# One layer of a hybrid decoder: q and k groups as plain block products, branch sums collected in DRAM by adding DMAs, a new order of the seven products

## The chip, the cores and the metric

The kernel runs on one core of a Trainium2 chip. The metric is device time in microseconds (us) of one execution. The kernel before was timed three times: 840.45, 841.55 and 841.84 us, a median of 841.55 us.

A core has five engines that run their own instruction streams and wait for each other by semaphores: TensorE (PE in the profile; its weight loads are listed apart as PEld), VectorE (DVE), ScalarE (ACT), GpSimd (POOL) and SyncE (SP), which here only issues DMAs. Matmuls write PSUM, of which the kernel uses eight banks of 128 partitions x 512 fp32 values: four for the dense products (pool `pp`) and four for everything else (pool `pa`). The inputs, the weights and the output lie in DRAM; all else is in SBUF.

## The reference

The input is 512 tokens of width 1024 with 16 learned meta tokens ahead. One layer, with batch 1, then a final norm:

```
u = rms_norm(h)                              # 528 tokens x 1024
rq, rk, rv, rg, gq, gk, gv, gg, glr, m_ret, m_gla = split(u @ w_in)
# retention, 4 heads: q, k of 256, v of 512
o_ret = group_norm(retention(rope(rq), rope(rk) / 16, rv)) * silu(rg)
# gated linear attention, 4 heads: q, k of 128, v of 256
log_a = log_sigmoid(glr @ w_gate_up + b_gate) / 16
o_gla = rms_norm(gla(gq / sqrt(128), gk, gv, log_a)) * silu(gg)
merged = sigmoid(m_ret) * (o_ret @ w_branch_ret) + sigmoid(m_gla) * (o_gla @ w_branch_gla)
out = rms_norm(h + merged @ w_out)           # the 16 meta positions dropped
```

All of it is fp32. The wide products are u @ w_in (1024 x 11,280), the two branch products and w_out.

## The kernel before

**Splits.** TensorE multiplies fp32 values that are rounded to a shorter form (`fp32r`). To keep the accuracy, every operand is split in two parts, hi and lo: ScalarE writes hi as a rounded copy and VectorE writes lo = value - hi (`split`, lines 139-141). One product then takes three matmuls, hi*hi, hi*lo and lo*hi (`mm3`, lines 143-146, and the inner loop of `quad`, line 221).

**quad (lines 186-273).** Most groups of w_in columns are computed two 256-column blocks at a time, for both halves of the tokens, with seven block products in place of eight (Strassen's scheme in Winograd's form). Products are numbered 1 to 7; each is 24 matmuls. The token side of the seven (two plain blocks of u, sums of blocks, ...) is split once and kept: `fh[0..6]` and `fl[0..6]`. The weight side needs block sums that VectorE makes in place (lines 251, 252, 253, 259), and then a split. A product accumulates in a PSUM bank, b, a or c, and intermediate values are copied out of bank b by ScalarE (`copy`, line 228, tiles `*_x1` to `*_x3`) before the next product adds to that same bank. The order is 1 2 7 6 5 3 4: b gets 1, then 6, then 5, then 3. Between 6 and 5, and between 5 and 3, no other product stands on TensorE. VectorE adds the copies to the banks in the evacuation.

The q and k columns of a head (of a pair of heads in the gated part) are done `wide`: the matrix of weights is stationary, the tokens move, and the result is transposed. There the meta tokens ride along, so that each matmul moves 264 columns (256 tokens and 8 meta tokens), and a product has two banks. There are six such calls: gq0, gq1 and rq0 to rq3.

**Stages.** In order: norm and transposes of u (`xt`, line 411); gv0 (`proj_b`, with 512 columns a matmul); gq0 with the forget gates woven in (glr, z, la); gg0 with the attention of the first pair of gated heads; gq1; gv1; gg1 and the branch product bg0 (`branch`) with the attention of the second pair; bg1. Then for each retention head h: rq (woven with the attention of head h-1, tiles av, on, sg, ot), the branch product br of head h-1, rg woven with the scores (sc), and rv. At the end the gates mr0, mr1 (woven with the attention of head 3), mg0, mg1, then br3 and w_out.

**weave (from line 156).** It alternates one step of a dense generator (a product) with one step of a chain generator (attention). `ret_attention` has the steps values 0, 1, 2, turn 0, values 3, turn 1. `values(ib)` makes 128 tokens of the output (av), its norm on VectorE, GpSimd and ScalarE, and multiplies it into sg (line 874). `turn` transposes two such blocks on TensorE (ot, line 337), which reads sg.

**What sets the order.** The program is written as above, but a framework orders the instructions of each engine itself by a cost model, subject to the data dependences. In the kernel before it may move matmuls of one product ahead of others, and it does at some places.

**Buffers.** Raw weights, hi and lo parts have small rings (three for hi and lo); SyncE issues a weight load when its buffer is free. `acc` holds the sum of the gated branch in SBUF (1024 x 512 fp32, 16 KB a partition), `acc2` that of the retention branch. VectorE adds each branch product to them (lines 720 and 931). The gated sum goes to DRAM (`kept`) and is read back for the gates (`kp`). The gates: VectorE and ScalarE form the sigmoid, VectorE multiplies (906, 917), GpSimd adds to acc2 (918), and br3 adds the last product to it on VectorE (935).

## Time and profile before

| what | value |
|---|---|
| runs of the kernel before | 840.45, 841.55, 841.84 us |
| the profiled execution: time, span of its trace | 841.58 us, 839.8 us |
| granted TensorE clock, mean | 0.988 of full speed |
| PE busy | 784.0 us (93% of the span), 5322 matmuls |
| DVE, ACT, POOL busy | 619.5, 422.8, 133.7 us |
| DMA engines busy | 30%, 78.82 MB moved |
| gv0 begins, gq0 begins, gg0 begins | 11.1, 43.7, 82.2 us |
| TensorE begins to wait for turn 0 of head 0, 1, 2 | 367.8, 472.8, 578.0 us |

How to read it: the page gives busy time by engine, then the span in 40 slices with the TensorE clock that was granted, then the chain of work that ended last, then groups of instructions by line, then DMAs. In a row of groups or of the timeline stand the start, the duration, the engine, the line of the kernel, the operation, the tile written and the tiles read, the shape, and in brackets how long the engine had been idle and who released it. Matmuls overlap: a matmul of 256 columns is shown as 0.28 us long, but the next starts 0.12 us after it, so the cost of a row of matmuls is read from one start to the next.

### The profile page before, as it was taken

To read this page: it belongs to the slowest core of one execution; us is meant where nothing else is said; L and a number is where in the kernel's file an instruction comes from. 1 tells how busy PE (TensorE), PEld (TensorE's weight loads), DVE (VectorE), ACT (ScalarE), POOL (GpSimd) and SP (SyncE) were. 2 spreads that over 40 slices of the span, in tenths; PEclk is the share of its full clock that TensorE was granted. 3 is DMA by queue.
4 is the path that set the end of the run, shared out by engine and by line. 5 is a ranking of instruction groups with operands and counts; after the bars stand their busy time and mean duration, and the time that the engine had idled before them with its cause. 6 is when DMAs were issued, how large, how long until landed. Compare 5 with 4: busy or idle time off the path is not lost. (4 is left out here: it accounts for less than half of the span.)

```text
span 839.8 us, 13348 instructions
## 1 busy us (share of the span) xinstructions
PE 784.0 (93%) x5322; PEld 703.9 (84%) x5322; DVE 619.5 (74%) x893; ACT 422.8 (50%) x707; POOL 133.7 (16%) x170
## 2 busy tenths in 40 slices
PE   7987989999899989999999999999999998989996
PEld 4777888898787978987999879998799998888886
DVE  3889686777637698887677887788877877887822
ACT  6665775456742445545445443454434555454422
POOL 4500332022400130022000220002200000032031
PEclk8998999999999999999999999999999999999999
DMA  8212211224122504242222422224222236335202
GB/s 278 84 56 76 76 45 54 66 90 126 52 75 100 177 25 127 77 125 75 69 81 79 126 76 64 81 83 127 76 64 82 82 105 208 114 103 176 73 1 101
DMA packets 72390, 78.82 MB, mean 94 GB/s; under 512 B 6964, under 2 KB 64564, under 8 KB 72328
## 3 DMA queue, kind: packets, MB, share of 16 engines
q1 hardware_dynamic: 72328, 77.97, 30.5%
q8 instruction: 42, 0.69, 0.3%
q14 instruction: 20, 0.16, 0.1%
HBM read 73.77 MB, written 4.19 MB: 93 GB/s over the span
## 5 line engine op out<-in xcount | busy, mean ns | idle before, releaser
L152 POOL TENSOR_TENSOR g_r<-g_v,mhalf 128x1 f32<-128x1 f32 x16 | 10.1, 630 | 305.7 <-DVE g_v L151 305.7
L144 PE MATMUL br_p<-oh,br_h 128*128 128x512 f32 x128 | 50.7, 401 | 1.0 <-ACT br_h L140 1.0
L145 PE MATMUL br_p<-ol,br_h 128*128 128x512 f32 x128 | 50.3, 396 | 0.0
L146 PE MATMUL br_p<-oh,br_l 128*128 128x512 f32 x128 | 50.1, 395 | 0.0
L140 ACT CAST rg_h<-rg_w 128x1024 fp32r<-128x1024 f32 x24 | 25.3, 1052 | 45.8 <-PE br_p L145 24.2
L140 ACT CAST rq_h<-rq_w 128x1024 fp32r<-128x1024 f32 x24 | 25.3, 1053 | 34.4 <-PE bg_p L145 13.0
L221 PE MATMUL rv_b<-rv_h,fh 128*128 128x256 f32 x128 | 37.0, 289 | 3.5 <-ACT rv_x L228 3.5
L221 PE MATMUL rq_b<-fh,rq_h 128*128 128x264 f32 x128 | 36.9, 288 | 1.0 <-ACT rq_x L228 1.0
L141 DVE TENSOR_TENSOR rg_l<-rg_w,rg_h 128x1024 fp32r<-128x1024 f32 x24 | 29.3, 1221 | 11.3 <-ACT rg_h L140 11.3
L221 PE MATMUL rg_b<-rg_h,fh 128*128 128x256 f32 x128 | 36.6, 286 | 0.9 <-DVE rp L760 0.9
L221 PE MATMUL rq_b<-fh,rq_l 128*128 128x264 f32 x128 | 36.6, 286 | 0.0
L221 PE MATMUL rq_b<-fl,rq_h 128*128 128x264 f32 x128 | 36.3, 283 | 0.0
L221 PE MATMUL rv_b<-rv_l,fh 128*128 128x256 f32 x128 | 36.0, 281 | 0.0
L221 PE MATMUL rg_b<-rg_l,fh 128*128 128x256 f32 x128 | 36.0, 281 | 0.0
L221 PE MATMUL rv_b<-rv_h,fl 128*128 128x256 f32 x128 | 36.0, 281 | 0.0
L221 PE MATMUL rg_b<-rg_h,fl 128*128 128x256 f32 x128 | 35.9, 281 | 0.0
L141 DVE TENSOR_TENSOR rv_l<-rv_w,rv_h 128x1024 fp32r<-128x1024 f32 x24 | 29.0, 1222 | 8.0 <-ACT rv_h L140 7.8
L141 DVE TENSOR_TENSOR rq_l<-rq_w,rq_h 128x1024 fp32r<-128x1024 f32 x24 | 30.4, 1266 | 3.9 <-ACT rq_h L140 3.9
L140 ACT CAST rv_h<-rv_w 128x1024 fp32r<-128x1024 f32 x24 | 24.8, 1053 | 12.2 <-DVE rv_w L252 5.6
L144 PEld LDWEIGHTS br_p<-oh,br_h 128*128 128x128 f32 x128 | 23.8, 188 | 8.2 <-ACT br_h L140 1.2
L221 PEld LDWEIGHTS rv_b<-rv_h,fh 128*128 128x128 f32 x128 | 24.1, 188 | 7.3 <-ACT rv_x L228 6.1
L145 PEld LDWEIGHTS br_p<-ol,br_h 128*128 128x128 f32 x128 | 24.1, 188 | 5.9
(478 smaller groups left out, 3062.1 us busy)
## 6 DMA issues: line engine op xcount, KB each, us to landing
rq_w<-in_w_in_dram SPq DMA_DIRECT2D x16, 512.0 KB, 3.7
rg_w<-in_w_in_dram SPq DMA_DIRECT2D x16, 512.0 KB, 3.6
rv_w<-in_w_in_dram SPq DMA_DIRECT2D x16, 512.0 KB, 3.7
br_w<-in_w_branch_ret_dram SPq DMA_DIRECT2D x16, 512.0 KB, 3.4
gv_w<-in_w_in_dram SPq DMA_DIRECT2D x8, 512.0 KB, 7.4
gq_w<-in_w_in_dram SPq DMA_DIRECT2D x8, 512.0 KB, 4.0
gg_w<-in_w_in_dram SPq DMA_DIRECT2D x8, 512.0 KB, 3.8
bg_w<-in_w_branch_gla_dram SPq DMA_DIRECT2D x8, 512.0 KB, 3.5
```

The source lines that it names most:

```text
L140: nc.scalar.copy(hi, src)
L141: eng.tensor_sub(lo, src, hi.bitcast(F32))
L144: nc.tensor.matmul(o, lh, rh, start=first, stop=False)
L145: nc.tensor.matmul(o, lh, rl, start=False, stop=False)
L146: nc.tensor.matmul(o, ll, rh, start=False, stop=last)
L152: nc.gpsimd.tensor_tensor(r[:rows], v[:rows], mhalf[:rows], op=ALU.pow)
L221: nc.tensor.matmul(ps, l, r, start=first and j == 0, stop=last and j == 2, skip_group_check=not fresh or (t == 1 and not wide))
```

## The change

It has five parts.

1. **q and k groups.** The six wide calls of `quad` become two calls each of a new function, `proj_a`: plain block products, four (two halves of the depth by two halves of the tokens), each for two 128-column tiles and 4 x 3 matmuls, 96 matmuls for the 256 columns of q and 96 for those of k. q moves 256 columns (no meta tokens), k 264. Two weight splits for each in place of seven for both; no block sums, no copies out of PSUM, no adds. The rope reads the PSUM banks directly, for q in one set of 512-column operations.
2. **Order of the products in quad.** 1 2 6 7 5 4 3 in place of 1 2 7 6 5 3 4. The third intermediate is copied from bank c after product 7, no longer from b after 5. The second block sum is now t2.
3. **Order on TensorE.** `pin` ties the first matmul of each dense group to the last one of the group before (no semaphore, order only). Dense groups (gv, quad, proj_a, branch, w_out) then stand in program order; matmuls of the chains may still be placed between.
4. **Branch sums.** acc and acc2 go away. ScalarE copies each branch product out of PSUM, and a DMA stores it (the first term, by SyncE) or adds it in DRAM (later terms, by GpSimd with `accum_op=add`) to `kept` or `kept2`. 32 adding DMAs of 256 KB: 8 in bg1, 16 in br1 and br2, 8 in mg. In mr the sum is read, multiplied and written back; in mg `kept` is read, multiplied and added; in br3 `kept2` is read. GpSimd's scratch for descriptors grows from 1024 to 4096.
5. **Smaller ones.** In ret_attention both turns come after all four values. The forget gates use other buffers, and their last logarithm is five operations of 512 columns in place of one of 2560. The temporary ring `tmp` has 7 buffers in place of 6, the second pool of the gated part is gone, and the splits of one block of u stay all through.

The diff, cut:

```diff
+    order = []
+    def pin(ins):
+        if order:
+            tc.add_manual_dep(ins.ins, order[0].ins.name, mybir.DependencyInfo(
+                mybir.DependencyClass.NoSync, mybir.DependencyReason.DATA), reason="order of products")
+    def mm3(o, lh, ll, rh, rl, first, last, dense=False):
+        m = nc.tensor.matmul(o, lh, rh, start=first, stop=False)
+        if dense:
+            pin(m)
         nc.tensor.matmul(o, lh, rl, start=False, stop=False)
-        nc.tensor.matmul(o, ll, rh, start=False, stop=last)
+        m = nc.tensor.matmul(o, ll, rh, start=False, stop=last)
+        if dense:
+            order[:] = [m]
...
+        b, a, c = [ppt(f"{name}_{x}").rearrange("p (t c) -> p t c", t=2) for x in "bac"]
+        def product(i, form, w, ps, fresh):
             hi, lo = wsplit([P, 4, 256], f"{name}_{i}")
             split(hi, lo, w)
...
+                        if t == kk == j == 0:
+                            pin(m)
+            order[:] = [m]
 
...
-        product(1, A11, blk[0, 0], "b", True)
-        x1 = copy("b", 1)
+        product(1, A11, blk[0, 0], b, True)
+        x1 = copy(b, 1)
         run_late()
         yield
         t2 = wraw(f"{name}_t2")
-        product(2, A12, blk[1, 0], "a", True)
+        product(2, A12, blk[1, 0], a, True)
         nc.vector.tensor_sub(blk[0, 0], blk[0, 1], blk[0, 0])
+        nc.vector.tensor_sub(t2, blk[1, 1], blk[0, 0])
+        evac(0, 0, a, x1)
+        yield
+        product(6, S2, t2, b, False)
+        x2 = copy(b, 2)
         nc.vector.tensor_sub(blk[0, 1], blk[1, 1], blk[0, 1])
-        nc.vector.tensor_sub(t2, blk[1, 1], blk[0, 0])
-        out(0, 0, "a", x1)
-        yield
-        product(7, S3, blk[0, 1], "c", True)
-        yield
-        product(6, S2, t2, "b", False)
+        yield
+        product(7, S3, blk[0, 1], c, True)
+        x3 = copy(c, 3)
         nc.vector.tensor_sub(blk[1, 0], blk[1, 0], t2)
-        x2 = copy("b", 2)
         if meta is not None:
             late.append(lambda: meta(psm))
         yield
-        product(5, S1, blk[0, 0], "b", False)
-        out(1, 1, "c", copy("b", 3))
+        product(5, S1, blk[0, 0], b, False)
+        evac(1, 1, b, x3)
         run_late()
         yield
-        product(3, S4, blk[1, 1], "b", False)
-        out(1, 0, "b", None)
-        yield
-        product(4, A22, blk[1, 0], "c", False)
-        out(0, 1, "c", x2)
-        yield
+        product(4, A22, blk[1, 0], c, False)
+        evac(0, 1, c, x2)
+        yield
+        product(3, S4, blk[1, 1], b, False)
+        evac(1, 0, b, None)
+        yield
+    def proj_a(col, meta, name, evac):
+        if meta:
+            pss = [[ppt(f"{name}_p{t}{th}")[:, :HT] for th in range(2)] for t in range(2)]
+        else:
+            full = [ppt(f"{name}_p{t}") for t in range(2)]
+            pss = [[p[:, th * 256:(th + 1) * 256] for th in range(2)] for p in full]
+        n = HT if meta else 256
+        for kh in range(2):
+            raw = wraw(f"{name}_w{kh}")
+            hi, lo = wsplit([P, 4, 256], f"{name}_{kh}")
+            nc.sync.dma_start(raw, w_in[kh * 512:kh * 512 + 512, col:col + 256].rearrange("(k p) c -> p k c", p=P))
+            split(hi, lo, raw)
+            for th in range(2):
+                for t in range(2):
+                    c = slice(t * P, t * P + P)
+                    for kk in range(4):
+                        a = [f[th, kh][:, kk, :n] for f in (ah, al)]
+                        first = kh == kk == 0 and (meta or th == 0)
+                        for j, (l, r) in enumerate(((hi, a[0]), (hi, a[1]), (lo, a[0]))):
+                            m = nc.tensor.matmul(pss[t][th], l[:, kk, c], r, start=first and j == 0,
+                                                 stop=kh == 1 and kk == 3 and j == 2,
+                                                 skip_group_check=not meta and th == 1)
+                            if t == kk == j == 0:
+                                pin(m)
+                order[:] = [m]
+                if meta and kh == 1:
+                    evac(th, [pss[t][th] for t in range(2)])
+                run_late()
+                yield
+        if not meta:
+            evac(full)
...
-        def evac(n, th, t, x, y):
-            if n == 1:
-                total(k[:, t, th, :], x, y)
-            else:
-                total(q[:, t, th * 256:(th + 1) * 256], x[:, :256], y if y is None else y[:, :256])
-        yield from quad((C_GQ + p * 256, C_GK + p * 256), False, f"gq{p}", evac, wide=True)
+        def evac_q(ps):
+            for t in range(2):
+                nc.scalar.copy(q[:, t, :], ps[t])
+        def evac_k(th, ps):
+            for t in range(2):
+                nc.vector.tensor_copy(k[:, t, th, :], ps[t])
+        yield from proj_a(C_GQ + p * 256, False, f"gq{p}", evac_q)
+        yield from proj_a(C_GK + p * 256, True, f"gk{p}", evac_k)
...
+    def collect(dst, t, first):
+        if first:
+            nc.sync.dma_start(dst, t)
+        else:
+            nc.gpsimd.dma_start(dst, t, accum_op=ALU.add)
 
     def gla_branch(p):
         def evac(c, ps):
-            if p == 0:
-                nc.scalar.copy(acc[:, c, :], ps)
-            else:
-                nc.vector.tensor_add(acc[:, c, :], acc[:, c, :], ps)
-                nc.sync.dma_start(kept[:, c, :], acc[:, c, :])
+            t = gp.tile([P, 512], F32, tag="gb", name=f"gb{p}{c}", bufs=2)
+            nc.scalar.copy(t, ps)
+            collect(kept[:, c, :], t, p == 0)
 
...
-        yield from quad((C_RQ + h * 256, C_RK + h * 256), False, f"rq{h}", evac, wide=True)
+        def evac_q(ps):
+            rope(ps, cs[:, 0, :, :256], cs[:, 1, :, :256], [qh[:, i, :] for i in range(2)],
+                 [ql[:, i, :] for i in range(2)], f"rpq{h}")
+        def evac_k(th, ps):
+            rope(ps, cs[:, 0, th, :], cs[:, 1, th, :], [kh[:, i, th, :] for i in range(2)],
+                 [kl[:, i, th, :] for i in range(2)], f"rpk{h}{th}")
+        yield from proj_a(C_RQ + h * 256, False, f"rq{h}", evac_q)
+        yield from proj_a(C_RK + h * 256, True, f"rk{h}", evac_k)
...
...
-        values(2)
-        yield
-        turn(sg, 0, oh, ol, rgain, h * 4, f"ot{h}")
-        yield
-        values(3)
-        yield
-        turn(sg, 1, oh, ol, rgain, h * 4, f"ot{h}")
-        yield
+        for ib in range(NTB):
+            values(ib)
+            yield
+        for half in range(2):
+            turn(sg, half, oh, ol, rgain, h * 4, f"ot{h}")
+            yield
...
+        def part(dst, src, g, name, first):
+            k = tmp2(name)
+            nc.sync.dma_start(k, src)
+            nc.vector.tensor_mul(k, k, g)
+            collect(dst, k, first)
...
-                a = acc2[:, 4 * j + 2 * n:4 * j + 2 * n + 2, s]
-                nc.vector.tensor_mul(a, a, g)
...
+                part(kept2[:, d, s], kept2[:, d, s], g, f"kr{j}{n}{th}", True)
...
-                nc.vector.tensor_mul(g, g, k)
-                nc.gpsimd.tensor_add(acc2[:, d, s], acc2[:, d, s], g)
...
+                part(kept2[:, d, s], kept[:, d, s], g, f"kg{j}{n}{th}", False)
...
     def ret_branch(h):
         def evac(c, ps):
-            if h == 0:
-                nc.scalar.copy(acc2[:, c, :], ps)
-            elif h < 3:
-                nc.vector.tensor_add(acc2[:, c, :], acc2[:, c, :], ps)
+            t = tmp(f"mt{h}{c}")
+            if h < 3:
+                nc.scalar.copy(t, ps)
+                collect(kept2[:, c, :], t, h == 0)
             else:
-                t = tmp(f"mt{c}")
+                k = tmp(f"mk{c}")
+                nc.sync.dma_start(k, kept2[:, c, :])
                 nc.vector.tensor_mul(t, sigr[c // 2][:, c % 2, :], ps)
-                nc.vector.tensor_add(t, t, acc2[:, c, :])
+                nc.vector.tensor_add(t, t, k)
                 split(mh[c // 2][:, c % 2, :], ml[c // 2][:, c % 2, :], t)
```

What the change does to the order of instructions, at three places.

**TensorE at the start.** Rows of TensorE's stream: xt0 to xt4 are the transposes of the five token blocks (the fifth is the meta tokens); gv0_p0 to p3 are the first product's four token tiles, and gv0_0, gv0_1, gv0_2 are consecutive quarters of its weights. Before, from the last matmul of p1 with the first quarter on (six matmuls of p1 with the second quarter follow these rows):

```order
L146 MATMUL gv0_p1_337<-gv0_0_h_341,fl0_87 128x512
L145 MATMUL gv0_p0_336<-gv0_1_l_372,fh0_80 128x512
L146 MATMUL gv0_p0_336<-gv0_1_h_371,fl0_87 128x512
L144 MATMUL gv0_p0_336<-gv0_1_h_371,fh0_80 128x512
L145 MATMUL gv0_p0_336<-gv0_1_l_372,fh0_80 128x512
L146 MATMUL gv0_p0_336<-gv0_1_h_371,fl0_87 128x512
```

Now, from the same place:

```order
L156 MATMUL gv0_p1_334<-gv0_0_h_338,fl0_87 128x512
L444 MATMUL xt2_0_214<-ident_71,xn2_212 128x128 x4
L444 MATMUL xt2_1_222<-ident_71,xn2_212 128x128 x4
L152 MATMUL gv0_p2_335<-gv0_0_h_338,a21h_101 128x512
L444 MATMUL xt3_0_239<-ident_71,xn3_237 128x128 x4
L444 MATMUL xt3_1_247<-ident_71,xn3_237 128x128 x4
L155 MATMUL gv0_p2_335<-gv0_0_l_339,a21h_101 128x512
```

The matmuls with the second quarter no longer stand ahead of the transposes of the third token block. Counted to the transposes xt4, 36 matmuls of gv0 stood ahead before and 19 stand there now.

**ScalarE in mg1.** ScalarE's stream, in which every product shows as the cast of its weights (mg1_1_h for product 1), with the copies out of PSUM between. Before:

```order
L140 CAST mg1_6_h_7958<-mg1_t2_7889 128x1024
L228 COPY mg1_x1_7887<-mg1_b0_7862 128x512
L140 CAST mg1_5_h_7989<-mg1_w00_7850 128x1024
L894 ACTIVATE mg100_7924<-mg100_7924 128x512
L140 CAST mg1_3_h_8026<-mg1_w11_7856 128x1024
L140 CAST mg1_4_h_8060<-mg1_w10_7852 128x1024
L228 COPY mg1_x2_7987<-mg1_b0_7862 128x512
L140 CAST br3_0_h_8110<-br3_0_w_8109 128x1024
L228 COPY mg1_x3_8017<-mg1_b0_7862 128x512
```

Now:

```order
L140 CAST mg1_7_h_7936<-mg1_w01_7830 128x1024
L140 CAST mg1_5_h_7967<-mg1_w00_7826 128x1024
L929 ACTIVATE mg100_7898<-mg100_7898 128x512
L140 CAST mg1_4_h_8002<-mg1_w10_7828 128x1024
L234 COPY mg1_x2_7933<-mg1_b_7834 128x512
L140 CAST mg1_3_h_8037<-mg1_w11_7832 128x1024
L234 COPY mg1_x3_7964<-mg1_c_7836 128x512
L140 CAST br3_0_h_8086<-br3_0_w_8085 128x1024
L929 ACTIVATE mg111_7995<-mg111_7995 128x512
```

All three copies came out of bank b; now the third comes out of bank c. x2 is copied while product 7 runs in bank c, and x3 while product 5 runs in b; the copies stood between two products of the same bank before.

**TensorE in rq1.** The second turn of head 0 (ot0_10 and ot0_11, each four transposes). Before, it stood in the last product of the wide quad (rq1_4):

```order
L221 MATMUL rq1_c1_3831<-fl2_89,rq1_4_h_4066 128x264
L221 MATMUL rq1_c1_3831<-fh2_82,rq1_4_l_4067 128x264
L337 MATMUL ot0_10_4048<-ident_71,sg0_3143 128x128 x3
L337 MATMUL ot0_11_4057<-ident_71,sg0_3143 128x128 x3
L221 MATMUL rq1_c1_3831<-fh2_82,rq1_4_h_4066 128x264
```

Now it stands in the middle of the k group:

```order
L297 MATMUL rk1_p11_3899<-a21l_102,rk1_0_h_3901 128x264
L297 MATMUL rk1_p11_3899<-a21h_101,rk1_0_l_3902 128x264
L372 MATMUL ot0_10_3972<-ident_71,sg0_3131 128x128 x4
L372 MATMUL ot0_11_3981<-ident_71,sg0_3131 128x128 x4
L297 MATMUL rk1_p00_3896<-fh1_81,rk1_1_h_3991 128x264
```

Between the last matmul of av03 and the second turn stood 42 matmuls of products 3 and 4 before; now there are 48 of the k group and the first turn. Between av01 and the first turn there were 48 matmuls of rq1, and now there are 72.

More of the change, by code (lines that the diff above doesn't have):

```diff
@@ L184, in wsplit, with quad @@
                 wp.tile(shape, F32R, tag="wlo", name=f"{name}_l", bufs=3))
-    def quad(cols, rows, name, evac, meta=None, wide=False):
+    def quad(cols, rows, name, evac, meta=None):
         blk = {}
@@ L199, in quad @@
                                   .rearrange("(k p) c -> p k c", p=P))
-        n_tok = HT if wide else 512
-        banks = {}
-        def bank(x):
-            banks[x] = [(pat if wide and x == "a" else ppt)(f"{name}_{x}{t}") for t in range(2 if wide else 1)]
-        def product(i, form, w, x, fresh):
+        b, a, c = [ppt(f"{name}_{x}").rearrange("p (t c) -> p t c", t=2) for x in "bac"]
+        def product(i, form, w, ps, fresh):
             hi, lo = wsplit([P, 4, 256], f"{name}_{i}")
@@ L219, in product @@
                     for j, (x1, x2) in enumerate(((0, 0), (0, 1), (1, 0))):
-                        l, r = (a[x1], b[x2]) if rows else (b[x1], a[x2])
-                        nc.tensor.matmul(ps, l, r, start=first and j == 0, stop=last and j == 2,
-                                         skip_group_check=not fresh or (t == 1 and not wide))
+                        l, r = (u[x1], v[x2]) if rows else (v[x1], u[x2])
+                        m = nc.tensor.matmul(ps[:, t, :], l, r, start=first and j == 0, stop=kk == 3 and j == 2,
+                                             skip_group_check=not fresh or t == 1)
@@ L224, in copy @@
+                        if t == kk == j == 0:
+                            pin(m)
+            order[:] = [m]
         def copy(x, n):
-            y = xc.tile([P, 2, HT] if wide else [P, 512], F32, tag="xc", name=f"{name}_x{n}")
-            for t in range(2 if wide else 1):
-                nc.scalar.copy(y[:, t, :] if wide else y, banks[x][t][:, :n_tok])
-            return y
-        def out(n, th, x, y):
-            for t in range(2 if wide else 1):
-                p = banks[x][t][:, :n_tok]
-                q = y[:, t, :] if y is not None and wide else y
-                evac(n, th, t if wide else None, p, q)
+            y = xc.tile([P, 2, 256], F32, tag="xc", name=f"{name}_x{n}")
@@ L237, in quad @@
+            nc.scalar.copy(y, x)
+            return y
         if meta is not None:
@@ L498, in forget_gates @@
                 yield
-        nc.scalar.activation(acc[:, :5, :], acc[:, :5, :], AF.Ln, bias=one)
         for b in (4, 0, 1, 2, 3):
-            nc.vector.tensor_sub(la[:, b, :], la[:, b, :], acc[:, b, :])
+            ln = nc.scalar.activation(es[b], es[b], AF.Ln, bias=one)
+            tc.add_manual_dep(ln.ins, last.ins.name, mybir.DependencyInfo(
+                mybir.DependencyClass.NoSync, mybir.DependencyReason.DATA), reason="one table after the other")
+            nc.vector.tensor_sub(la[:, b, :], la[:, b, :], es[b])
         yield
```

127 lines of the change are left out of this document (52 added, 75 removed).

## The prediction

> **What bounds the kernel now.** I read the page, then a table of windows, then TensorE's waits, then the timeline where they point.
>
> ```profile
> span 839.8 us, 13348 instructions
> PE 784.0 (93%) x5322; PEld 703.9 (84%) x5322; DVE 619.5 (74%) x893; ACT 422.8 (50%) x707; POOL 133.7 (16%) x170
> ```
>
> TensorE is busy in 784.0 us and idle in 55.8; no other engine passes 74%. The time is TensorE's work plus its stops. The windows (columns: stretch, its length, busy time of PE, PEld, DVE, ACT, POOL, granted clock, DMA) tell where the stops are:
>
> ```profile
> 60.00:80.00 20.00, 14.95 (x103) 14.58 (x104) 18.46 (x29) 12.29 (x16) 0.00 (x0) 0.83 0.27 79
> 80.00:280.00 200.00, 190.83 (x1270) 171.62 (x1269) 138.31 (x218) 114.09 (x232) 43.40 (x49) 0.99 0.26 76
> 280.00:660.00 380.00, 363.56 (x2616) 331.51 (x2615) 298.61 (x440) 179.39 (x272) 43.93 (x60) 1.00 0.30 90
> 660.00:790.00 130.00, 120.99 (x873) 112.83 (x874) 108.11 (x135) 66.52 (x89) 16.59 (x12) 1.00 0.42 130
> ```
>
> Idle are 5.1 us in gq0 with VectorE nearly full (18.5 of 20), 9.2 in the rest of the gated part, 16.4 in retention, 9.0 in the gates. The waits of TensorE (us in total, times, longest) name the causes:
>
> ```profile
> PE ot L337 <- DVE sg L874: 10.1, 7, 1.8
> PE gq_b L221 <- DVE gq_l L141: 5.1, 1, 5.1
> PE rv_b L221 <- ACT rv_x L228: 3.5, 8, 0.7
> ...
> PE mg_b L221 <- ACT mg_x L228: 3.1, 2, 1.6
> ...
> PE mg_b L221 <- ACT mg_h L140: 2.1, 2, 1.1
> PE mr_b L221 <- ACT mr_x L228: 1.9, 2, 1.5
> ...
> PE rq_b L221 <- ACT rq_x L228: 1.0, 1, 1.0
> PE br_p L144 <- ACT br_h L140: 1.0, 1, 1.0
> ```
>
> **Term 1, the q and k groups: more work.** The cost of a matmul is the distance of starts. 24 of 256 columns, from the first of bank a to the first of bank c, and 24 of 264, from the first of rq to the first of av:
>
> ```profile
> 437.10 0.28 PE L221 MATMUL rv_a<-rv_h,fh 128*128 128x256 f32 x1
> 439.94 0.28 PE L221 MATMUL rv_c<-rv_h,fh 128*128 128x256 f32 x1
> 456.02 0.28 PE L221 MATMUL rq_b<-fh,rq_h 128*128 128x264 f32 x1
> 458.92 0.39 PE L144 MATMUL av<-vh,sh 128*128 128x512 f32 x1
> ```
>
> That is 2.84 and 2.90 us, or 0.118 and 0.121 each. A wide call is 168 x 0.121 = 20.3 us; its successor 96 x 0.118 + 96 x 0.121 = 23.0. Six calls add 6 x 2.66 = **+16.0 us** on the engine that bounds. VectorE loses per call three splits, four block sums and the adds, ScalarE three casts and six copies; that shortens nothing where they are not late.
>
> **Term 2, stops of order.** The rows with x1 to x3 (L228) are one thing: a product adds to bank b while ScalarE still copies b. The new order puts a product in another bank between every copy and the next write of that bank, 2.84 us against a copy of 512 columns, some 0.7 (as VectorE's statistics of that width in term 3). The mg_h and br_h rows are the next group's first matmuls, moved ahead of a product that must end before their weight buffer is free; kept in order they come after it. These rows sum to 3.5 + 3.1 + 2.1 + 1.9 + 1.0 + 1.0 = 12.6 us in 16 stops.
>
> A stop costs a little more than its idle time:
>
> ```profile
> 445.62 0.40 PE L353 MATMUL rvm_s<-rvm_h,sel 128*128 128x512 f32 x1
> 445.86 0.40 PE L354 MATMUL rvm_s<-rvm_l,sel 128*128 128x512 f32 x1
> 446.46 0.39 PE L221 MATMUL rv_b<-rv_h,fh 128*128 128x256 f32 x1 [0.21 <-ACT rv_x L228]
> ```
>
> The second start is 0.24 after the first, the third 0.60 after the second: 0.36 lost, 0.21 of it shown idle, so some 0.16 a stop for the pipe to fill again. 12.6 + 16 x 0.16 = **-15.2 us**. This part follows from the order alone; I keep 11 as its lower bound (mg_h and br_h staying).
>
> **Term 3, the turns.** VectorE at the second turn of head 1:
>
> ```profile
> 483.08 0.53 DVE L141 TENSOR_TENSOR kl<-rp,kh 128x264 fp32r<-128x264 f32 x1 [1.09 <-ACT kh L140]
> ...
> 484.16 0.69 DVE L867 BATCH_NORM_STATS2 b<-av 128x6 f32<-128x512 f32 x1
> 486.98 1.21 DVE L874 TENSOR_TENSOR sg<-on,sg 128x512 f32<-128x512 f32 x1 [0.22 <-ACT on L873]
> ```
>
> The statistics of av03 stand behind a lo part of k for which VectorE idled 1.09 us (it waits for the rope on GpSimd), and from the statistics to the end of sg it is 4.0 us. Now the statistics stand ahead of q's rope, and of the rope two multiplies of 512 columns (0.69 each, as the statistics) stand ahead of sg: 4.0 + 1.4 = 5.4 us after av03. The turn comes 48 x 0.121 = 5.8 us and the first turn's eight transposes after av03, so it finds sg ready; the first turn has 24 matmuls and av03 more than that. So **-10.1 - 7 x 0.16 = -11.2 us**; bound, half of it staying. Late next is the second pair of banks that the k group takes over from q's rope: the first of them is wanted 24 x 0.121 = 2.9 us and the first turn after av03, and is read before sg's multiply starts, 2.8 + 1.4 = 4.2 us after it. The eight transposes must take 1.3 us to hide that. It is the tightest place; a miss is under 1 us a head, and I cost it at nothing.
>
> **Term 4, gq0 and the forget gates.**
>
> ```profile
> 68.73 0.59 PE L221 MATMUL gq_b<-fh,gq_l 128*128 128x264 f32 x1 [5.05 <-DVE gq_l L141]
> 69.11 0.42 PE L221 MATMUL gq_b<-fh,gq_h 128*128 128x264 f32 x1
> 69.33 0.42 PE L221 MATMUL gq_b<-fl,gq_h 128*128 128x264 f32 x1
> ...
> 70.00:72.00 2.00, 2.00 (x11) 2.00 (x11) 1.56 (x3) 0.64 (x2) 0.00 (x0) 0.50 0.93 279
> ```
>
> After an idle 5.05 us the pitch is 0.22, not 0.12: the granted clock is half until 72 at least. The stop cost 5.1 + (72 - 68.7) / 2 = 6.7 us. It goes, since the late split is no longer there (**-6.7**). But the gates still take their time:
>
> ```profile
> 54.84 1.17 PE L488 MATMUL z<-fg_r 128*128 128x512 f32 x4
> 71.77 0.41 ACT L140 CAST lah<-la 128x256 fp32r<-128x256 f32 x1 [1.36 <-DVE la L501]
> ```
>
> From z to lah are 16.9 us. VectorE loses two splits and two adds in this stretch and gains one split, about 2 us by the split's 1.23 (row in the rivals). The first matmuls of the attention (ge, gf), which need lah, now stand four matmuls into k0. From z TensorE needs 85 x 0.118 for the rest of q, 4 x 0.121, 1.2 for the z and three more matmuls of 0.24: 12.4 us. 16.9 - 2 - 12.4 = **+2.5 us**, a new stop, between 0 and 4.5. Term 4 is -4.2 in all; bounds -6.7 and, if the clock falls again, 0.
>
> **Term 5, the start.** Before the last transposes 36 matmuls of gv0 stood ahead, now 19:
>
> ```profile
> 17.99 0.56 PE L146 MATMUL gv_p<-gv_h,fl 128*128 128x512 f32 x1
> 18.39 0.40 PE L144 MATMUL gv_p<-gv_h,fh 128*128 128x512 f32 x1
> ```
>
> The transposes wait for norms and input, not for TensorE, so 17 x 0.24 = 4.1 us of work moves behind them. Here too the clock is slow at first (0.56 long) and full from 18.39 on (0.40). With more idle time it may come later, at up to the 1.6 us of term 4: I take 0.9. **+5.0 us**, bounds 0 and 6. [...]
>
> **Edits costed at nothing.** The adds on VectorE and GpSimd become ScalarE copies of 512 columns, at most 0.7 us by the statistics of that width, beside 12 matmuls of 0.24 a chunk, 2.9 us; if that cover were gone they would cost 0.7 each. An adding DMA is not in the trace. The nearest rows:
>
> ```profile
> kept<-acc SPq DMA_DIRECT2D x8, 256.0 KB, 2.2
> kp<-kept SPq DMA_DIRECT2D x8, 256.0 KB, 4.8
> ```
>
> A store landed in 2.2 us, a load with a busy queue in 4.8; an add reads and writes, so at most about 7. I take 5. In bg1 two buffers alternate, so a chunk may take (0.7 + 5) / 2 = 2.85 us, just its matmuls; three spare banks cover 8.7 us more. In br1 and br2 seven buffers cover 20 us. After the last mg product the add, then a read, come to 0.7 + 0.7 + 5 + 4.8 = 11 us; br3 needs that chunk after six others, 17 us. The gated attention's 9.2 us of stops stay.
>
> **Sum.** 841.6 + 16.0 - 15.2 - 11.2 - 4.2 + 5.0 = 832.0, on the profiled execution of 841.58 us, which is the median of the runs (841.55): **832 us**.
>
> **Rivals.**
> *The moved work costs nothing (17%).* Terms 4 and 5 without their costs: 832 - 5.0 - 2.5 = 824.5. For it: VectorE was nearly full in 60:80, so the end of gq0 may hang on it and not on when TensorE begins. Against: the change itself takes work off VectorE there.
>
> *The block sums come late (12%, slower).* The third product used to be 7, now it is 6, and its weights need t2, one sum more, with two others ahead of its split.
>
> ```profile
> 436.71 1.23 DVE L141 TENSOR_TENSOR rv_l<-rv_w,rv_h 128x1024 fp32r<-128x1024 f32 x1
> ```
>
> The split ended at 437.94, the third product began at 439.94: 2.0 us of slack, 0.8 after one sum more (as long as the split). With three operations of 0.69 in between, as where attention is woven in, it is 1.3 + 0.16 late. There are 15 such quads: 15 x 1.4 = 21, so 853 us. It decides from 0.8 us of delay on. Against it: VectorE is relieved ahead of most of them.
>
> *Adding DMAs are slow (8%, slower).* At 10 us each, bg1 needs (0.7 + 10) / 2 = 5.35 us a chunk, 8 x 2.45 - 8.7 = 11 us late, and as br1 and br2 are covered, 843. It decides from about 7 us.
>
> *Half of terms 2 and 3 comes back as other stops (10%).* 832 + 13 = 845; a third of it gives 841, no change.
>
> **How the numbers follow.** The forecast (825 to 839) has 53%. A measurement of this kernel can tell 0.2%, 1.7 us. Faster by more than that: 53 + 17 and 3 of the last rival, 73%; within it 7% (last rival); slower 20%. The range 820 to 846 leaves out a part of the first rival and most of the second, under 2 in 10.
>
> **What would show it.** PE with about 5,466 matmuls and 16 us more work. No waits on L234 copies, none of ot on sg; a wait of ge on lah near 67 us. The start of gq0 at 48 to 53 us. Retention heads of 105.2 us (turn 0 to turn 0 of heads 0 and 1) at 105 + 2.7 - 1.2 - 3.7 = 103 us (term 1, two x stops, two turns). Waits of quads on `_l` at product 6 would be the second rival; waits on gb, kg or mk the third.

## The result, and the profile after

The changed kernel takes **822.6 us** (median of 4 runs, 821.34 to 823.74) against 841.69 us (840.45 to 842.98) for the kernel before on the same chip: a ratio of 0.977, 95% interval 0.975 to 0.979. The prediction was 832.0 us, range 820 to 846. The time lies inside, 9.4 us below the forecast, and is nearest to the rival "the moved work costs nothing" (824.5). That is chance: by this rival gg0 would have begun 4.0 us earlier than before (3.5 - 5.0 - 2.5), and it began 3.8 us later.

The page of the changed kernel (time 823.74 us in this profiled execution):

```profile
span 822.0 us, 13635 instructions
PE 790.3 (96%) x5466; PEld 719.3 (88%) x5466; DVE 541.5 (66%) x775; ACT 407.7 (50%) x673; POOL 147.3 (18%) x186
```

There are 5,466 matmuls as foretold, but PE's busy time grew by 6.3 us, not by 16. The busy time counts every moment that lies in at least one record, and records overlap: one of 256 columns lasts 0.28 us, the next starts 0.12 us after it, and one behind a stop or at half the clock is longer still (0.39 us at 686.48, 0.42 at 690). So it is a poor measure of added work. Idle time of TensorE fell from 55.8 to 31.7 us. The windows, with the columns of those shown of before:

```profile
60.00:80.00 20.00, 16.31 (x110) 15.85 (x109) 17.68 (x26) 10.07 (x16) 0.00 (x0) 0.83 0.10 29
80.00:280.00 200.00, 194.15 (x1325) 175.75 (x1324) 116.92 (x195) 113.29 (x226) 51.02 (x55) 1.00 0.35 96
280.00:660.00 380.00, 380.00 (x2830) 356.75 (x2829) 267.99 (x371) 177.84 (x258) 53.69 (x71) 1.00 0.39 103
660.00:790.00 130.00, 124.21 (x831) 113.23 (x831) 97.11 (x124) 61.44 (x82) 12.85 (x11) 0.99 0.67 191
```

In retention (third row) TensorE has no idle time left at all; VectorE lost 30.6 us of work there. Of TensorE's waits that remain, these four bear on the prediction (us in total, times, longest):

```profile
PE mr_b L225 <- DVE mr_l L141: 2.4, 1, 2.4
PE ge L624 <- ACT lah L140: 2.4, 1, 2.4
PE wo_p L152 <- DVE mt L974: 2.0, 3, 1.3
...
PE gk_p L297 <- DVE gk_l L141: 1.3, 1, 1.3
```

The waits on x copies, on sg, on mg_h and br_h are gone. New are ge on lah, which term 4 named; a wait in mr1 on the late split, which is rival 2 in one quad out of fifteen; one of gq0's k group on its late split; and w_out on mt, the multiplies that read the banks of br3.

The next table shows where the time went. A stage is counted from its first matmul in the timeline to that of the next stage; the last column is from the first matmul of mr0 to the last matmul of w_out.

| us | start, gv0, gq0 | gg0 to bg1 | retention | gates, br3, w_out |
|---|---|---|---|---|
| before | 82.2 | 193.0 | 391.0 | 166.9 |
| predicted change | +3.5 | +2.7 | -6.5 | -9.2 |
| changed | 86.0 | 188.8 | 375.3 | 165.0 |
| measured change | +3.8 | -4.2 | -15.7 | -1.9 |

(The predicted changes are the terms laid out by place: one wide call is +2.66 in the first two columns each and four are in the third, with the turns and the rv_x and rq_x stops; the stops at mr_x, mg_x, mg_h and br_h are in the last.) The start was right to 0.3 us, in one profile: in five profiles of programs with that same start, gg0 began at 83.5 to 86.0 us, and the granted clock differs with it. In this one the mean clock in 60 to 80 us was 0.83 and gg0 began at 86.0; where it was 0.91 (a_sums and a_dvecopy below), at 83.7 and 83.5. The second column and retention gained 7 and 9 us more than said, the last column 7 us less.

### The profile page after: what moved, and what is told of

Its sections match the earlier page's. It is cut to its first block, busy times and chain, and to the rows that moved or that the text cites. A ratio compares the mean times of both kernels' runs of the same rounds, so it can differ in the third digit from the quotient of the medians.

```text
span 822.0 us, 13635 instructions
## 1 busy us (share of the span) xinstructions
PE 790.3 (96%) x5466; PEld 719.3 (88%) x5466; DVE 541.5 (66%) x775; ACT 407.7 (50%) x673; POOL 147.3 (18%) x186
## 4 chain that ended last, share of the span: by engine, by line
PE 75%; DVE 6%; DMA 4%; ACT 4%; issue 2%; POOL 2%; SPq 0%; POOLq 0%; DVEq 0%; ACTq 0%
PE rk_p L297 6%; PE rg_b L225 6%; PE rq_p L297 6%; PE rv_b L225 5%; PE gk_p L297 3%; PE rg_c L225 3%; PE br_p L155 3%; PE br_p L152 3%; PE br_p L156 3%; PE rv_c L225 2%; PE mg_b L225 2%; DMA mk<-kept 2%; PE gg_b L225 2%; PE wo_p L152 2%; PE wo_p L156 2%
## 5 line engine op out<-in xcount | busy, mean ns | idle before, releaser
L914 ACT ACTIVATE on<-av,nm,g_r 128x512 f32<-128x512 f32 x16 | 12.5, 778 | 52.6 <-DVE nm L912 52.6
L639 POOL COPY gto<-gX 128x1 f32<-128x1 f32 x16 | 8.5, 530 | 122.9 <-ACT gX L629 122.9
L638 POOL TENSOR_TENSOR gQ<-gX,gq 128x512 f32<-128x512 f32 x16 | 28.3, 1768 | 3.9 <-ACT gX L631 3.9
L152 PE MATMUL wo_p<-wo_h,mh 128*128 128x512 f32 (+1 forms) x72 | 26.9, 374 | 2.0 <-DVE mt L974 2.0
L156 PEld LDWEIGHTS br_p<-oh,br_l 128*128 128x128 f32 x128 | 24.0, 188 | 5.2
L297 PE MATMUL rk_p<-fh,rk_h 128*128 128x264 f32 x96 | 27.6, 287 | 0.0
```

What stands on the lines that cost most here:

```text
L152: m = nc.tensor.matmul(o, lh, rh, start=first, stop=False)
L156: m = nc.tensor.matmul(o, ll, rh, start=False, stop=last)
L297: m = nc.tensor.matmul(pss[t][th], l[:, kk, c], r, start=first and j == 0, stop=kh == 1 and kk == 3 and j == 2, skip_group_check=not meta ...
L638: nc.gpsimd.tensor_mul(Q[b, h], X[:, 0:4, :], qb)
L639: nc.gpsimd.tensor_copy(TO[b, h], X[:, 0, P - 1:P])
L914: nc.scalar.activation(on, ps, AF.Identity, scale=r, bias=nm)
```

## The experiments

Theory A at the outset was the prediction's: order on TensorE takes the stops away, and q and k as plain products cost 16 us for it. Rival B: the stops go because VectorE and ScalarE are relieved, whatever the order.

### Order without the new q and k, and q and k undone

b_order is the kernel before with the three edits of order:

```diff
+ pin(...)                    # dense groups tied on TensorE, wide quads too
- product order 1 2 7 6 5 3 4
+ product order 1 2 6 7 5 4 3
- values 0 1 2, turn 0, values 3, turn 1
+ values 0 1 2 3, turn 0, turn 1
```

> The kernel before with the order parts alone: dense groups kept in order on TensorE, products 1 2 6 7 5 4 3 (in the wide quads too), turns after all four values. q and k stay wide quads, the sums stay in SBUF. Theory A, the order took the stops away: 841.7 - 15.2 (terms 2) - 11.2 (term 3) + 5 (start), so about 820, with no waits on x copies and none of ot on sg. Rival B, the relief of VectorE did it (fewer splits, no block sums for q and k, no adds): the turns and the stops in gq0 stay, 833 or more.

a_wide is the changed kernel with its six q and k groups back in the wide form (in the new order, tied):

```diff
- yield from proj_a(C_RQ + h * 256, False, f"rq{h}", evac_q)
- yield from proj_a(C_RK + h * 256, True, f"rk{h}", evac_k)
+ yield from quad_wide((C_RQ + h * 256, C_RK + h * 256), f"rq{h}", evac)   # and gq
```

> The changed kernel with part 1 undone: q and k again by wide quads of seven products, in the new order and kept in order; everything else as changed. Theory A: TensorE has 16.0 us less work and the stops stay away but for gq0's late split (about 5 to 7 us): 822.6 - 16 + 6 = 813, so that the q and k part by itself is a loss. Rival B: three splits, four sums and the adds per call go back to VectorE, the turns and gq0 wait again: 822 or more.

Measured: b_order **846.1 us** (ratio 1.006, 1.004 to 1.008), a_wide **851.3 us** (1.013, 1.010 to 1.015). Both are slower than the kernel before. Of b_order's three edits the order of products alone (b_prod, below) took 830.4 us, so the tie and the late turns cost 15.7 us there. Theory A falls as far as q and k go: undoing the part that was booked as a cost of 16 us made the kernel 28.7 us slower. TensorE's waits and the timeline in a_wide, at the branch product of head 0:

```profile
PE sc L152 <- ACT kh L140: 15.4, 4, 4.2
```

```profile
380.31 0.50 PE L152 MATMUL br_p<-oh,br_h 128*128 128x512 f32 x1 [1.01 <-ACT oh L410]
381.95 0.80 PE L155 MATMUL br_p<-ol,br_h 128*128 128x512 f32 x1 [1.13 <-DVE ol L411]
386.90 0.79 PE L152 MATMUL sc<-qh,kh 128*128 128x512 f32 x1 [4.15 <-ACT kh L140]
...
389.20 0.63 PE L152 MATMUL br_p<-oh,br_h 128*128 128x512 f32 x1
389.62 0.63 PE L155 MATMUL br_p<-ol,br_h 128*128 128x512 f32 x1
```

The wide quad has seven steps to weave with six of attention, so the last turn ends just before the branch product, which waits for the turn's oh and ol (3.1 and 3.4 us in three heads). The scores of the next head, which no tie holds, stand two matmuls into the branch product and wait 4.15 us for k's rope, which comes last in the wide form. The matmuls after it start 0.42 apart instead of 0.23. The branch product takes 31.8 us (first of br to first of rg), 22.0 in the changed kernel.

To tell the tie from the wide form, a_widenopin takes the tie out of a_wide:

```diff
-        if order:
+        if False:
             tc.add_manual_dep(ins.ins, order[0]
```

> The changed kernel with q and k back to wide quads (new order of products) and without the tie on TensorE. With the tie this kernel took 851.3 us: the scores, which the tie leaves free, stood in the branch product ahead of their data and held TensorE, with the clock at half after. Theory A, the tie makes that loss (it keeps other dense matmuls from standing there): 838 us or less. Rival B, the wide form makes it, since the last turn and k's rope come just before the branch product whatever the order: 846 or more.

Measured: **840.0 us** (ratio 0.9985, 0.997 to 0.9999). It lies between the two expectations: 11 us of a_wide's loss belong to the tie, the rest to the wide form as it stands with late turns. Its largest stops stand at the branch products, on the rope, oh and ol:

```profile
PE br_p L152 <- DVE rp L834: 7.0, 3, 2.3
PE br_p L155 <- DVE ol L411: 3.4, 3, 1.1
PE br_p L152 <- ACT oh L410: 3.1, 3, 1.1
```

Without a tie, q and k as plain products are worth 840.0 - 817.3 = 22.8 us (817.3 is a_nopin, below), with it 28.7.

### The order of the products alone

a_oldorder is the changed kernel with products 1 2 7 6 5 3 4 again; b_prod is the kernel before with the new order and nothing else.

```diff
  product(1) product(2)
- product(6) product(7) product(5) product(4) product(3)
+ product(7) product(6) product(5) product(3) product(4)     # a_oldorder; b_prod the reverse
```

> The changed kernel with the old product order 1 2 7 6 5 3 4 (third copy out of bank b), still kept in order on TensorE. Theory A: the 15.2 us of term 2 come back but for mg_h and br_h (3.1 us and their restarts, which the kept order covers), and the late block sum in mr1 goes (some 4 us): +11.6 - 4, about 830, with waits on x2 and x3 in rv, mr and mg. Rival B: ScalarE and VectorE are freer, so the copies come in time: within 4 us of 822.6.

> The kernel before with the new order of the seven products (1 2 6 7 5 4 3) and nothing else. Theory A, the x copies of term 2 go with the order alone: 3.5 + 3.1 + 1.9 + 1.0 us in 14 stops, with 0.16 each for restart 11.7 us: 829 to 831. Rival B, the wide quads leave VectorE no room, the sum t2 that product 6 now needs as the third product comes late (rival 2 of the prediction): 838 or more, with waits of product 6 on its split.

Measured: a_oldorder **836.3 us** (0.995, 0.993 to 0.996), b_prod **830.4 us** (0.989, 0.987 to 0.992). TensorE's waits in a_oldorder:

```profile
PE mg_b L225 <- ACT mg_x L234: 6.1, 4, 1.6
PE rv_b L225 <- ACT rv_x L234: 3.5, 8, 0.7
...
PE mr_b L225 <- ACT mr_x L234: 3.1, 2, 1.5
```

The order alone is worth 10.9 us before and 13.7 us in the changed kernel. The eight rv_x stops come back with the very 3.5 us of before. Term 2 stands. In b_prod the stops on sg stay, larger than before:

```profile
PE ot L338 <- DVE sg L875: 12.1, 7, 2.1
```

### The turns

a_oldturn is the changed kernel with the turns where they were:

```diff
-        for ib in range(NTB):
-            values(ib)
-        for half in range(2):
-            turn(half)
+        values(0); values(1); values(2); turn(0); values(3); turn(1)
```

> The changed kernel with the old steps of the attention of a retention head: values 0, 1, 2, turn 0, values 3, turn 1. Theory A (the distance on TensorE took the waits away): +11, about 833, waits of ot on sg in every head. Rival B (VectorE's rope of k in the old wide quad was what came late): under 3 us more, about 824.

Measured: **823.0 us** (0.979, 0.977 to 0.980), no change. Four stops on sg came back:

```profile
PE ot L372 <- DVE sg L915: 4.8, 4, 1.3
```

Retention is 4.1 us longer (379.4), and mr0 and mr1 are 3.8 us shorter (50.8 against 54.6 from the first matmul of mr0 to that of mg0): the stop in mr1 is gone. So late turns do what term 3 said, at a third of its size, and pay it back in mr1, where in the changed kernel the turn's operations and the block sums stand ahead of product 6's split on VectorE:

```profile
682.69 0.87 DVE L380 SCALAR_TENSOR_TENSOR ol<-ot,rgain,oh 128x256 fp32r<-128x256 f32 x2
...
684.08 1.22 DVE L252 TENSOR_TENSOR mr_t<-mr_w,mr_w 128x1024 f32<-128x1024 f32 x1
685.22 1.22 DVE L257 TENSOR_TENSOR mr_w<-mr_w,mr_w 128x1024 f32<-128x1024 f32 x1
686.35 1.22 DVE L261 TENSOR_TENSOR mr_w<-mr_w,mr_t 128x1024 f32<-128x1024 f32 x1
...
688.09 1.21 DVE L141 TENSOR_TENSOR mr_l<-mr_t,mr_h 128x1024 fp32r<-128x1024 f32 x1
```

Of this row of sums only the one at 684.08 is needed by product 6; those at 685.22 and 686.35 belong to later products.

### The sums behind the split

a_sums holds those two sums behind product 6's split:

```diff
+        behind(nc.vector.tensor_sub(blk[0, 1], blk[1, 1], blk[0, 1]), low)   # low: the split's lo of product 6
+        behind(nc.vector.tensor_sub(blk[1, 0], blk[1, 0], t2), low)
```

> The changed kernel with two block sums of each quad (the ones for products 7 and 4) held behind the split of product 6 on VectorE, so that only the two sums that product 6 itself needs stand ahead of it. Aimed at the one stop of the rival 'block sums come late', in mr1: 0.93 and 2.52 us idle at 685.4 and 686.7, then the clock at 0.75 for 5 us. Theory A, the stop is queueing on VectorE and goes: 0.9 + 2.5 + 1.2 = 4.6 us off, 818 us. Rival B, VectorE is full there and the wait moves to product 7 or 5: 821 to 824. Rival C, the sums come too late for product 7 in the heads too: above 825.

Measured: **821.9 us** (0.978, 0.975 to 0.980): not told apart from the changed kernel. The gates were 3.7 us shorter in its profile (161.3 us), but a new wait came in the gated attention, where gg0 to bg1 took 2.0 us more (190.7; a_dvecopy, which has no edit there, took 190.3, so this column is uncertain by 1.5 us):

```profile
PE gm L673 <- DVE lal L141: 3.3, 2, 1.9
...
PE mr_c L225 <- DVE mr_l L141: 1.2, 1, 1.2
```

The time is the one that rival B named, and so is one of the waits: the row of mr_c is product 7 waiting for its own split. The stop before product 6 did shrink (mr_b on mr_l, 2.4 to 0.8 us), so the place was right. The edit hits all quads, and only mr1 had the stop; an edit of mr1 alone was not run.

### What the added matmuls cost

a_short leaves out 12 of the 96 matmuls of each q and k group, so that TensorE has 5,322 as before:

```diff
                         for j, (l, r) in enumerate(((hi, a[0]), (hi, a[1]), (lo, a[0]))):
+                            if j == 1 and kh == 0 and kk < 3:
+                                continue
```

> The changed kernel with 12 of the 96 matmuls of each q and each k group left out (the hi*lo term of three quarters of the first half of the depth), so that TensorE has 5,322 matmuls as before; nothing else is changed, and q and k lose that small term. Measures what term 1 costs. Theory A, q and k work lies fully on the path: 144 x 0.119 = 17 us off, 805 to 806 us. Rival B, part of it was cover for VectorE and ScalarE, and stops take its place: 810 us or more, with waits on ge, sc or ot that the full kernel lacks.

Measured: **810.4 us** (0.963, 0.961 to 0.965). The 144 matmuls cost 12.2 us, not 17.1, as rival B said. By stage against the changed kernel: gg0 to bg1 -2.8 (one call, in full), retention -9.5 (of 11.4), gates +3.4, where br3 waits 1.2 us more for VectorE (mt) and mg 0.5 for a late split; the rest of the 3.4 was not told apart. In gq0 only 1.1 came out of 2.8: the wait for the gates is 1.0 longer, and the clock in 60 to 80 us was 0.74 in this profile against 0.83.

```profile
PE ge L626 <- ACT lah L140: 3.4, 1, 3.4
```

### The tie on TensorE alone

a_nopin is the changed kernel without the tie (the edit of a_widenopin).

> The changed kernel without the tie between dense groups on TensorE (part 3 undone, all else as changed). With q and k as plain products the planner then moves instructions at three places only: the start (19 to 36 matmuls of gv0 ahead of the last transposes, as before), bg1 (the first matmuls of four chunks stand side by side) and mr1 (two matmuls of product 7 ahead of product 6). Theory A, the order costs 5.2 us at the start (gv0's end moved behind the transposes and the gates' first matmuls) and gives 1 to 2 us elsewhere: 818 to 820 us, gg0 beginning near 83 us. Rival B, the end of gq0 hangs on the gates and VectorE, so the start is nearly free: 821 to 824, gg0 beginning near 86 us in both. Rival C, the order itself carries the gain (terms 2 and 3): 830 or more.

Measured: **817.3 us**, the fastest kernel that leaves no work out, with 5.3 us less than the changed kernel (its own ratio 0.9719, 0.9705 to 0.9734, against 0.9773, 0.9751 to 0.9794). By stage: gg0 begins at 82.5 us, gg0 to bg1 is 1.4 shorter, and the gates are 1.9 shorter (two matmuls of product 7 fill mr1's stop); retention is the same to 0.1 us. With plain q and k, the tie changes nothing in retention, where it was to help, and costs at the start and in mr1. The stop of ge on lah remains there (2.9 us).

### The tail

In the changed kernel the last load of kg stands on SyncE's queue behind a load of w_out's weights that waits for its buffer:

```profile
741.72 0.46 SPq L938 DMA_DIRECT2D kg<-kept  x1
747.69 0.37 SPq L314 DMA_DIRECT2D wo_w<-in_w_out_dram  x1
748.15 0.57 SPq L938 DMA_DIRECT2D kg<-kept  x1
```

n_tail moves these loads to GpSimd's queue, on a_nopin:

```diff
-            nc.sync.dma_start(k, src)
+            (nc.sync if first else nc.gpsimd).dma_start(k, src)
...
-                nc.sync.dma_start(k, kept2[:, c, :])
+                nc.gpsimd.dma_start(k, kept2[:, c, :])
```

> The changed kernel without the tie on TensorE (817.3 us alone) and with the loads of kg (in mg) and mk (in br3) issued by GpSimd's queue, ahead of the adding DMAs in program order, instead of SyncE's, where they stand behind weight loads that wait for their buffers. Theory A, the late part of br3 and w_out comes from these loads: VectorE's wait of 4.9 us for the last kg goes, and with it TensorE's stops in w_out (0.5 + 1.4 + 0.5 idle and their restart, some 3 us): 814 to 815 us. Rival B, VectorE is the limit there (splits of weights and of the merged sum, multiplies) and idles for kg only because it is ahead: 816.5 to 818. Rival C, the loads are late on GpSimd as well, behind the issue of the adding DMAs (1.2 us each): above 818.5.

n_best adds the edit of a_sums to it.

> The changed kernel without the tie on TensorE, with the kg and mk loads on GpSimd's queue, and with the two block sums held behind the split of product 6. If the three gains add up (5.3 us measured for the tie, 3 estimated for the tail, and of the sums the 1.2 + 0.8 us of waits that mr1 still has without the tie): 812 us. If the sums only move the wait to the next product, as in the changed kernel itself, 814 to 816.

Measured: n_tail **821.4 us** (0.977, 0.976 to 0.979), 4.1 more than a_nopin; n_best **820.7 us** (0.976, 0.975 to 0.978), not told apart from n_tail and above both of its expectations; a_sums' new wait of gm on lal (3.3 us) is there too. n_tail's profile shows 2.5 of the 4.1 us, all of them from mr0 on. Rival C held, for a reason it half named. GpSimd in n_tail (in brackets its idle time and releaser):

```profile
741.65 1.24 POOL L759 DMA_DIRECT2D kept<-kg  x1 [6.96 <-DVE kg L939]
742.41 1.23 POOL L938 DMA_DIRECT2D kg<-kept  x1
```

An adding DMA waits for its multiply, and the next load stands behind it in the same stream: the load at 742.41 had GpSimd idle for 6.96 us before the adding DMA ahead of it. One queue with waits was exchanged for another. VectorE's longest wait for an mk grew from 0.8 to 3.6 us.

### Which engine reads PSUM in the branch products

96 matmuls of br took 22.58 us before (first to last start) and 21.76 now. a_dvecopy gives the copies out of PSUM back to VectorE:

```diff
-                nc.scalar.copy(t, ps)
+                nc.vector.tensor_copy(t, ps)
```

> The changed kernel with the branch products of heads 0 to 2 copied out of PSUM by VectorE instead of ScalarE; the adding DMAs stay. Measures why 96 matmuls of br take 21.98 us now and took 22.82 before (0.229 against 0.238 each). Theory X, the distance of starts depends on which engine reads PSUM beside the matmuls: with VectorE back at 0.238, +0.84 us a head, about 825 us. Theory Y, it belongs to something else (the sum that stood in SBUF, short stops that the records do not show): 0.229 stays and the time moves by less than 1.5 us unless VectorE's 24 copies of 0.7 us make new stops.

Measured: **822.8 us** (0.978, 0.976 to 0.980), the same. First and last matmul of br1 before, and in a_dvecopy:

```profile
489.69 0.40 PE L144 MATMUL br_p<-oh,br_h 128*128 128x512 f32 x1
512.27 0.39 PE L146 MATMUL br_p<-oh,br_l 128*128 128x512 f32 x1
```

```profile
478.24 0.39 PE L152 MATMUL br_p<-oh,br_h 128*128 128x512 f32 x1
500.00 0.39 PE L156 MATMUL br_p<-oh,br_l 128*128 128x512 f32 x1
```

21.76 us with VectorE too, so the reader of PSUM is not the cause. What cost 0.8 us a head before stays open; the add with its second operand in SBUF was not tried apart. No run takes the branch sums in DRAM (part 4) back by themselves, so their worth as a whole is open too.

## Why the prediction came out as it did

**Term 1 (+16.0).** This is the step that failed. As a count of work it holds: in gg0 to bg1, taking the 24 matmuls of one call out saves their 2.8 us in full. As the effect of the part it has the wrong sign: undone, the kernel is 28.7 us slower (22.8 without the tie). Both numbers are for the wide form with late turns. The fastest wide kernel here, b_prod with the old turns and the old branch sums, took 830.4 us; against it the changed kernel gains 7.8 us and a_nopin 13.1, with all their other parts. The wide form with the old turns was not run in the changed kernel, so the size of the gain is open between these numbers. The prediction wrote of the work taken off VectorE and ScalarE that it "shortens nothing where they are not late". They were late. TensorE waits for k's rope ahead of the scores (15.4 us in a_wide, 4.9 in b_prod) and for the last turn ahead of the branch product (6.5 us in a_wide), both costed at nothing, and for sg (12.1 us in b_prod), which the prediction put down to the place of the turns alone. In the order as it stands the price is 12.2 us by a_short.

**Term 2 (-15.2)** is right, at the lower end: -10.9 before (11.7 was expected of the x copies there), and -13.7 in the changed kernel, where the old order also spares the stop in mr1.

**Term 3 (-11.2).** The stops went, but not by the place of the turns, which gave 4.1 in the heads and lost 3.8 in mr1. The four cases: wide form with the old turns 12.1 us of stops (b_prod), wide form with late turns 13.5 at the branch products instead (a_widenopin), plain form with the old turns 4.8, plain form with late turns none. (b_prod has the old branch sums and gates too.) For the stops to go both parts are needed, and the larger share is that of q and k, which the prediction had not credited. The size of one stop was right: in the rows of before around head 1's first turn,

```profile
472.54 0.37 PE L221 MATMUL rq_b<-fh,rq_h 128*128 128x264 f32 x1
472.75 0.28 PE L221 MATMUL rq_b<-fl,rq_h 128*128 128x264 f32 x1
474.66 0.87 PE L337 MATMUL ot<-ident,sg 128*128 128x128 f32 x6 [1.64 <-DVE sg L874]
```

1.91 us pass from the second start to the third where a matmul takes 0.12: 1.79 lost, 1.64 + 0.16 foretold. The 0.09 between the first two beyond a matmul's 0.12 shows as no idle time at all: a delay shorter than the overlap of two records is in none of the sums.

**Retention** was to fall by 6.5 us and fell by 15.7. First turn to first turn of heads 0 and 1 is 101.72 us, foretold 103:

```profile
366.96 1.04 PE L372 MATMUL ot<-ident,sg 128*128 128x128 f32 x8
...
468.68 1.04 PE L372 MATMUL ot<-ident,sg 128*128 128x128 f32 x8
```

So heads 1 and 2 gained 1.3 us each more than said, 0.8 of it in the branch product. Half of the excess of the stage lies in head 0 alone: from the first matmul of rg0 to that of rv0 it took 31.3 us and takes 26.6. Two stops of before that went at this place were in its trace, and no term had them:

```profile
298.07 0.39 PE L221 MATMUL rg_b<-rg_h,fh 128*128 128x256 f32 x1 [0.85 <-DVE rp L760]
302.60 0.91 PE L144 MATMUL sc<-qh,kh 128*128 128x512 f32 x4 [1.30 <-ACT qh L140]
```

Both wait for the rope. The first ends where rg0 starts, so only the second counts in the 4.7 us, with 1.46 us; what the rest of them was is not told apart. The rope now reads PSUM directly, with no copies and adds ahead of it, and in the changed kernel no stop is left there.

**Terms 4 and 5 (-4.2, +5.0).** The sum to gg0 was +3.5 foretold against +3.8 in the profile, and the place was right: ge waits for lah from 67.4 us on, 2.36 us of it, where 2.5 was foretold. The agreement is in part luck. The clock fell again behind that stop, which term 4's bound allows and its sum does not:

```profile
69.75 0.39 PE L624 MATMUL ge<-gsum,lah 128*128 128x256 f32 x1 [2.36 <-ACT lah L140]
71.92 0.59 PE L297 MATMUL gk_p<-fh,gk_l 128*128 128x264 f32 x1 [1.33 <-DVE gk_l L141]
...
72.00:78.00 6.00, 6.00 (x27) 6.00 (x28) 5.96 (x6) 0.40 (x1) 0.00 (x0) 0.50 0.30 90
```

Some 6.2 us of dense matmuls at half pace are 3.1 us lost, where the stop of before cost some 2 in this way (half pace from 68.7 to 73.0). The wait of 1.33 us for the split was not foretold either. Against these, three stops of before in gq0 that no term had are gone (gq_c on gq_h and on gq_l, gq_a on gvm: 1.1, 0.5 and 1.3 us).

gq0 began at 53.7 us and not at 48 to 53: the 32 matmuls of glr, 3.9 us that stood inside gq0 before, stand ahead of it now. Less these, the last matmul of gv0 comes 6.1 us later than before in this profile and 4.9 to 5.2 later in the four others with the same start, where 5.0 was foretold. The two terms are not independent. The gates themselves began no later (z at 55.1 us, 54.8 before), and the end of gq0 hangs on them, much as the first rival said: 1.1 of 2.8 us came out when work was taken away, and the tie's cost at the start was 1.0 to 3.5 us (gg0 at 82.5 without it, 83.5 to 86.0 with it). The clock at the start shows in the first 40 us before, and of the changed kernel:

```profile
0.00:20.00 20.00, 14.34 (x50) 8.87 (x51) 7.23 (x12) 12.90 (x23) 8.74 (x17) 0.83 0.88 273
20.00:40.00 20.00, 19.55 (x101) 14.98 (x100) 16.41 (x20) 12.15 (x26) 10.24 (x15) 1.00 0.31 102
```

```profile
0.00:20.00 20.00, 13.83 (x50) 7.93 (x51) 7.24 (x12) 12.85 (x23) 9.09 (x18) 0.91 0.93 279
20.00:40.00 20.00, 17.27 (x80) 12.52 (x79) 15.72 (x20) 11.76 (x25) 9.83 (x14) 0.91 0.24 75
```

20 x (0.17 + 0) = 3.4 us of clock lost before, 20 x (0.09 + 0.09) = 3.6 now: the slow stretches are together no longer than before. But a part of them fell on an idle TensorE before. By the distance of starts, the matmuls of gv0 stood 0.43 us apart from 14.9 to 18.4 us before, and from 14.4 to 16.7 and from 27.0 to 30.5 now: (2.3 + 3.5 - 3.5) / 2, some 1.1 us more, near the 0.9 inside term 5. The second stretch is 3.5 us at half pace, 1.7 us lost.

**The second column** was to grow by one call and fell by 4.2 us. The gated attention's stops, which were to stay, went in part (9.2 us of idle TensorE in 80 to 280 us before, 5.9 now); b_prod, with the order of the products alone, has 189.9 there, 3.1 less than before. Where the rest went was not told apart.

**Edits costed at nothing.** The adding DMAs landed in 4.9 to 6.2 us by the medians of their three groups, 4.1 to 8.3 singly (5 was taken), and no branch product of bg1, br1 or br2 waits for a buffer. That part and its rival are settled. Three things were missed in the gates. First, the mr1 stop: the first matmul of product 6 starts at 686.48 and that of product 7 at 693.48, 7.0 us for 2.84 of work, and 0.9 before it. Second, the loads of kg and mk behind w_out's weights on SyncE's queue. Third, VectorE, whose multiplies of br3's banks with the gate (mt) are what w_out waits for. From br3 on the stage takes 4.3 us longer than before; a way to start these loads earlier that works was not found here.

**Rivals.** "The moved work costs nothing" came near with its number alone: terms 4 and 5 did have their costs. "Block sums come late" is true in one quad of fifteen, where chain work stands in front, and false in the others. "Adding DMAs slow" is false. "Half comes back as other stops" is true of the gates only.

## What to carry to other kernels

Before booking extra work on the bounding engine as a cost, list every stop of that engine which hangs on the work that the edit removes elsewhere, the small ones outside the main table too; here they outweighed 16 us of matmuls. An order that helps by hand at one place (products that change banks) can lose at another (dense groups tied, turns moved late), so each edit of order is timed alone. A load does not become early by changing its queue, if the new queue holds an instruction that waits for later data: in n_tail a load stood behind a wait of 6.96 us, and the kernel took 4.1 us more than a_nopin.

## What the runs showed of the hardware that was not expected

The granted clock fell behind stops much shorter than the 5.05 us of gq0 before. In a_wide two idle stretches of 1.01 and 1.13 us, with one matmul between them, stood ahead of the fall: the windows read 0.50 from 382 on, and the long stop of 4.15 us begins at 382.75.

```profile
378.00:382.00 4.00, 1.85 (x13) 1.33 (x11) 3.81 (x12) 2.63 (x6) 0.69 (x1) 0.96 0.00 0
382.00:384.00 2.00, 0.74 (x1) 0.23 (x1) 1.54 (x4) 1.60 (x5) 0.77 (x2) 0.50 0.00 0
...
390.00:392.00 2.00, 2.00 (x6) 1.56 (x5) 1.29 (x2) 0.00 (x0) 1.52 (x3) 0.52 0.59 144
392.00:394.00 2.00, 2.00 (x10) 1.60 (x10) 0.00 (x0) 0.59 (x1) 0.00 (x0) 1.00 0.63 220
```

In mr1 of the changed kernel stops of 0.77 and 2.37 us with two matmuls between stood ahead of it, and the half pace lasted from 689.35 to 692.51, 3.2 us of dense matmuls (the clock reads 0.50 in 690 to 692). That cost another 1.6 us behind 3.1 us of stops.
